# RWKV stage of a two-block network: small inverse blocks handled together, the identity added to a smaller tile, C's context left out, modulation slabs in fours

## The chip, the cores and the metric

The kernel runs on one core of a Trainium2 chip. The metric is the device time of one execution in microseconds (us): the median of three runs. Five engines work side by side, each through its own queue in order: TensorE (PE in the profile, its weight loads PEld), VectorE (DVE), ScalarE (ACT), GpSimd (POOL) and SyncE (SP), which here only issues loads of weights. They wait for one another by semaphores.

## The reference

Two transformer-like blocks over 512 tokens of width 1024, with a context of 256 tokens beside them. The first block normalises and modulates the tokens (a silu of `c` times `ada_w` gives six vectors: two for the first norm, four for later), multiplies tokens and context by one wide matrix `w_in`, and feeds the columns to two branches: an RWKV branch and a state-space branch (SSM). Then come a merge, a mixture of experts, and the second block. What the change touches:

```python
def step(s, inp):                       # rwkv_scan, for each token, 16 heads of 64, two directions
    r_t, w_t, k_t, v_t, kk_t, a_t = inp
    sa = jnp.einsum('bhvk,bhk->bhv', s, -kk_t)
    s = s * w_t[:, :, None, :] + sa[..., None] * (kk_t * a_t)[:, :, None, :] + v_t[..., None] * k_t[:, :, None, :]
    return s, jnp.einsum('bhvk,bhk->bhv', s, r_t)

# ssm_prep: convolution over x, B and C; C is read for outputs only
xbc = jax.nn.silu(dw_conv_centred(xbc, p['ssm_conv_w'], p['ssm_conv_b']))
xs, bm, cm = jnp.split(xbc, [SSM_DIM, SSM_DIM + SSM_BC], axis=-1)
```

The context gives states, no outputs: over it `rwkv_scan` and `ssd_chunked` are called with `with_output=False`, so C (`cm`) of the context enters nothing.

## The kernel before

**The RWKV branch** takes a chunk of 64 tokens at a time. Inside a chunk the state's correction is a triangular system, so each chunk, head and direction needs the inverse of a 64x64 unit-triangular matrix. There are 8 pairs of heads and 3 units a pair (context; tokens in two blocks, forward and backward in opposite order): 24 units of 16 matrices. A unit goes through three generators:

- `unit_in` prepares decays and the products AR and BK, multiplies them on PE (L1532), masks the result into G (L1537), **adds the identity to A's part of G, once for each direction (L1539)**, and writes A to a buffer in DRAM, `da`.
- `unit_inv` inverts. It reads the 64 diagonal 16x16 blocks of `da` back with one matrix to a partition (Ab), multiplies by a mask into Qb (L1571), and builds the inverse inside a partition on DVE for block sizes b = 2, 4 and 8: for each diagonal block a product (L1579) and a sum (L1581), twice over: four instructions for each of 8/b blocks. Then `Qb` goes through DRAM back to a layout for PE, and two more levels (16 to 32, 32 to 64) are done with matmuls (L1632, L1639, L1654, L1662). Between the first two of these, a mask `lv` (which holds the identity too) is multiplied onto the product: Yl (L1636).
- `unit_chain` runs the state through four chunks: for each, PE, then P (DVE, L1700), PE, W (ACT, L1708 and L1709), PE, then Sall (DVE, L1727).

**The order of the work.** PE's and SP's queues follow the order in which the program is written; on DVE, ACT and POOL a planner with costs of its own sorts. The program goes in 26 steps, numbered -2 to 23. Step i interleaves the chain of unit i, the inverse of unit i+1 and the inputs of unit i+2 with a list of fills, in 12 rounds; in each round every stream gives a twelfth of its work. A stream's work is the sum of what its `yield`s give, as a share of its weight:

```python
while at < n - 1 and sum(load[:at + 1]) >= total * (at + 1) // n:
    at += 1
steps[at].append(f(p))
load[at] += w
```

Fills, in order, with weights: 20 convolution tiles `conv_in` (24 each), the two halves of the remaining modulation `adaln_rest` (84 each), 5 more convolution tiles, and 16 gate tiles (16 each). The seven later head pairs (64 each) are bound to steps 0, 3, 6 and so on. A fill is mostly `in_proj`: for each of 8 slices of the contraction three matmuls of 512 columns (tokens; L202, L205 and L206, into `d`), and where the context is wanted three of 256 (into `dc`). Tiles 20 to 23 of `conv_in` are C.

**Modulation.** Each half has 32 matmuls (L1207) of a single weight column against a slab of 128x512 of `ada_w`. Four results share a PSUM bank, at partitions 0, 32, 64 and 96. A slab is loaded by SP (L1206) into a ring of five buffers `wr`, which the other fills use too. After each matmul comes a `yield 2.6`.

Of the kernel before, what the change touches and what calls it, by code (L numbers as in the profile page):

```python
# [15 lines left out]
AX = mybir.AxisListType  # L16
PSUM = bass.MemoryType.PSUM
P = 128
# [1014 lines left out]
L, CT = 512, 256  # L1033
N = L + CT
CH = 64
# [14 lines left out]
HE = [dict(A="",P="gpsimd",V="vector")[x] for x in "AAAP"]  # L1050
YS, YC, SG, SI, KS = 1.5, .6, 44, 20, 0
HQ = 6
EYE = 0
SH = 0
XA = 1

# [4 lines left out]
def host_consts1():  # L1061
    f = np.float32
    out = {}
    i = np.arange(P)
    p, t = i[:, None] % 64, np.arange(64)[None, :]
    one = lambda c: np.broadcast_to(c, (P, c.shape[1])).astype(f)
    out["rw"] = np.concatenate([one(p < t), one(p <= t), one(p > t), one(p >= t)], 1)
    out["eye2"] = one(p == t)
    pp, tt = i[:, None] % 32, np.arange(32)[None, :]
    lv = [(pp // 16 == 0) & (tt // 16 == 1) | (pp == tt), (pp // 16 == 1) & (tt // 16 == 0) | (pp == tt)]  # L1070
    out["lv"] = np.concatenate(lv, 1).astype(f)
    e = np.arange(16)
    out["q2"] = one(((e[:, None] == e[None, :]) | (e[:, None] % 2 == 0) & (e[None, :] == e[:, None] + 1)).reshape(1, 256))
    out["half16"] = np.stack([i // 16 % 2 == 0, i // 16 % 2 == 1], 1).astype(f)
    out["half32"] = np.stack([i // 32 % 2 == 0, i // 32 % 2 == 1], 1).astype(f)
    out["blk64"] = (i[:, None] // 64 == i[None, :] // 64).astype(f)
    k, j = i[:, None], i[None, :]
    for nm, m in (("le", k <= j), ("ge", k >= j), ("gt", k > j), ("lt", k < j)):
        out["m_" + nm] = m.astype(f)
    r = np.ones((1, 256), f)  # L1080
    r[:, ::CH] = 0
    out["rst"] = np.broadcast_to(r, (P, 256)).astype(f)
    return out
# [10 lines left out]
class Block1(Block2):  # L1094
# [100 lines left out]
    def adaln_rest(self):  # L1195

        nc, t = self.nc, self.t
        self.mod = self.dram.tile([8, 512], F32, name="mod")

        def half(p, h):  # L1200
            ps = self.pd.tile([P, 512], F32, name="d", bufs=2)
            for k in range(KC):
                for g in range(4):
                    w = self.raw()
                    c0 = 2048 + h * 2048 + g * 512
                    nc.sync.dma_start(w, t["ada_w"][0, k * P:(k + 1) * P, c0:c0 + 512])  # L1206
                    i = nc.tensor.matmul(ps[32 * g:32 * g + 1], self.sT[:, k, 0:1], w, start=(k == 0), stop=(k == KC - 1))  # L1207
                    if self.last is not None:
                        self.paced(i)
                    self.latest = i  # L1210
                    yield 2.6
            for g in range(4):
                m = p.tile([P, N + 3], F32, name="u", bufs=2)
                nc.scalar.copy(m[32 * g:32 * g + 1, :512], ps[32 * g:32 * g + 1])
                nc.gpsimd.dma_start(self.mod[h * 4 + g:h * 4 + g + 1], m[32 * g:32 * g + 1, :512])
        return [(84, lambda p: half(p, 0)), (84, lambda p: half(p, 1))]

    def bcast(self, out, ap, off, n, eng=None):
        (eng or self.nc.gpsimd).dma_start(out, bass.AP(tensor=ap.tensor, offset=ap.offset + off, ap=[[0, P], [1, n]]))
# [240 lines left out]
    def unit_in(self, p, q, pr, u, un):  # L1460

        nc, cs = self.nc, self.cs
# [10 lines left out]
        for j, src in enumerate((xw, xa)):  # L1473
            for d, ps in enumerate(pss):
                rd = slice(64 * d, 64 * d + 64)
                tk = slice(blocks[d] * U, (blocks[d] + 1) * U)
                i = nc.tensor.matmul(ps[:, j * U:(j + 1) * U], lw[rd, j], src[rd, tk], start=True, stop=True)
# [46 lines left out]
        G = p.tile([P, 2, 4, 2, 2, CH], F32, name="G", bufs=3)  # L1524
# [3 lines left out]
        for d in range(2):  # L1528
            pss = [q.tile([P, 4, 2, CH], F32, name="g", bufs=2) for _ in hs]
            for c in range(4):  # L1530
                for ps, r in zip(pss, hs):
                    i = nc.tensor.matmul(ps[:, c, :na], BK[r, d, c].rearrange("p s t -> p (s t)"),  # L1532
                                         AR[r, d, :na, c * CH:(c + 1) * CH], start=True, stop=True)
            self.mark(i)
            yield 4
            for h, ps in enumerate(pss):
                nc.vector.tensor_mul(G[:, d, :, h, :na], ps[:, :, :na], mk[:, d, None, :na].to_broadcast([P, 4, na, CH]))  # L1537
            Ad = G[:64, d, :, :, 0].rearrange("p c h t -> p (c h) t")
            (nc.gpsimd if EYE else nc.vector).tensor_add(Ad, Ad, self.k["eye2"][:64, None].to_broadcast([64, 8, CH]))  # L1539
            ps = q.tile([P, 4, P], F32, name="g", bufs=2)  # L1540
            for c in range(4):
                i = nc.tensor.transpose(ps[:, c], BK[:, d, c].rearrange("p s t -> p (s t)"), self.ident)
            self.mark(i)
            nc.scalar.copy(bk[:, d], ps)
            yield 2
# [15 lines left out]
    def unit_inv(self, p, q, pr, u, un, after):  # L1561
        nc = self.nc
# [5 lines left out]
        Ab, Qb, tm = AQ[:64, 0], AQ[:64, 1], AQ[64:].rearrange("p z a b -> p (z a b)")  # L1568
# [1 line left out]
        yield 1  # L1570
        nc.vector.tensor_mul(Qb, Ab, self.k["q2"][:64].rearrange("p (a b) -> p a b", a=16))  # L1571
        W = p.tile([P, 4, 32], F32, name="Vt")[:64].rearrange("p a b -> p (a b)")
        sq = lambda x, o, i, j, b: x[:, o + i:o + i + b, o + j:o + j + b]
        for b in (2, 4, 8):
            for o in range(0, 16, 2 * b):
                t4 = tm[:, :b * b * b].rearrange("p (i t j) -> p i t j", i=b, t=b)
                w = W[:, :b * b].rearrange("p (i t) -> p i t", i=b)
                for lhs, rhs, dst in ((sq(Ab, o, 0, b, b), sq(Qb, o, b, b, b), w), (sq(Qb, o, 0, 0, b), w, sq(Qb, o, 0, b, b))):
                    nc.vector.tensor_mul(t4, lhs[:, :, None, :].to_broadcast([64, b, b, b]),  # L1579
                                         rhs.rearrange("p j t -> p t j")[:, None].to_broadcast([64, b, b, b]))  # L1580
                    nc.vector.reduce_sum(dst, t4, axis=AX.X)  # L1581
            yield YJ
        nc.scalar.dma_start(view(db, 0, [[256, 64], [1, 256]]), Qb.rearrange("p a b -> p (a b)"))
        Qp = p.tile([P, 8, 16], F32, name="Qp")
# [4 lines left out]
        for d in range(2):  # L1589
            ps = q.tile([P, 2, P], F32, name="g", bufs=2)  # L1590
            for j in range(2):
                c = 4 * self.BLOCKS[u][d] + 2 * j
                i = nc.tensor.transpose(ps[:, j], pr.vT[:, c * CH:(c + 2) * CH], self.ident)
            self.mark(i)
            for b in range(2):
                o = V[64:, 3 - b::-2, d] if d else V[64:, b::2, d]
# [3 lines left out]
        ps = q.tile([P, 4, 2, CH], F32, name="g", bufs=2)  # L1600
        for n in range(4):
            for d, c in ((0, n), (1, 3 - n)):
                for h in range(2):
                    i = nc.tensor.matmul(ps[hs[h], n, d], un.G[64:, d, c, h, 0], V[64:, n, d, h], start=True, stop=True)
# [13 lines left out]
        H = 32  # L1618
# [9 lines left out]
        lv = self.k["lv"].rearrange("p (d t) -> p d t", d=2)  # L1628
        all_ = [(g, d, c) for d in range(2) for c in range(4) for g in range(4)]
        ps = q.tile([P, 2, 4, H], F32, name="t", bufs=1)  # L1630
        for a in all_:
            i = nc.tensor.matmul(pk(ps, *a), blk((T1, T0)[a[1]], *a), Qg(*a), start=True, stop=True)  # L1632
        self.mark(i)
        yield 2
        Yl = p.tile([P, 2, 4, H], F32, name="Yl")
        nc.vector.tensor_mul(Yl, ps, lv[:, :, None].to_broadcast([P, 2, 4, H]))  # L1636
        ps = q.tile([P, 2, 4, H], F32, name="t", bufs=1)
        for a in all_:
            i = nc.tensor.matmul(pk(ps, *a), Tg(*a), pk(Yl, *a), start=True, stop=True)  # L1639
# [100 lines left out]
    def spills(self):  # L1740

        nc = self.nc
        self.sg = self.dram.tile([16, P, L], F32, name="sg1")
        self.sz = self.dram.tile([16, P, L], F32, name="sz1")
        self.su = self.dram.tile([25, P, N], F32, name="su1")

        def stage(p):
            return p.tile([P, N + 3], F32, name="u", bufs=2)

        def gate(p, i, z):  # L1750
            def ev(ps):
                g = p.tile([P, L], F32, name="u", bufs=2)
                nc.scalar.activation(g, ps, AF.Tanh, scale=0.5)
                if z:
                    nc.vector.scalar_tensor_tensor(g, g, 1.0, ps, op0=OP.add, op1=OP.mult)
                else:
                    nc.vector.tensor_scalar(g, g, 0.5, 0.5, op0=OP.mult, op1=OP.add)
                nc.gpsimd.dma_start((self.sz if z else self.sg)[i], g)
            yield from self.in_proj((SS if z else GT) + i * P, P, ev)

        def conv_in(p, m):
            n = P if m < 24 else 64
            u = stage(p)[:, :N]
            yield from self.in_proj(SS + 2048 + m * P, n, lambda ps: nc.scalar.copy(
                u[:n, CT:].rearrange("p (c r) -> p c r", r=8), ps.rearrange("p (r c) -> p c r", r=8)),
                lambda ps: nc.scalar.copy(u[:n, :CT], ps))
            nc.gpsimd.dma_start(self.su[m, :n], u[:n])
        self.zs, self.gates = ([lambda p, i=i, z=z: gate(p, i, z) for i in range(16)] for z in (True, False))
        early = (self.zs + self.gates)[:NZ]
        self.late = (self.zs + self.gates)[NZ:]  # L1770
        return [(24, lambda p, i=i: conv_in(p, i)) for i in range(25)] + [(16, f) for f in early]


    def exp_small(self, p, x, name):
# [901 lines left out]
```

## Time and profile before

| | |
|---|---|
| median of 3 runs | 4425.99 us (4418.01 to 4428.55) |
| profiled execution: its own time | 4428.13 us |
| profiled execution: span | 4426.3 us |
| PE busy | 4059.9 us, 92% |
| DVE busy | 2266.0 us, 51% |
| ACT busy | 1576.9 us, 36% |
| POOL busy | 1005.9 us, 23% |
| mean granted TensorE clock | 0.961 |

The profile is one execution. In the windows of [rows 2] the first is the whole RWKV stage from the chain of unit 0 on, the others are steps 2, 5, 11, 13, 14 and 22, each from the first matmul of its chain to that of the next. A busy share counts the time in which an instruction of that engine ran; of the clock, the profile gives the share of full speed that TensorE was granted in a stretch. Line numbers are those of the kernel before. An fp32 matmul stands as two records in the trace, one for each pass.

### The profile page before, as it was taken

What the parts mean: (1) busy time and instruction counts of PE and PEld (TensorE: products, weight loads), DVE (VectorE), ACT (ScalarE), POOL (GpSimd) and SP (SyncE); (2) the same over time, 40 slices, a digit from 0 to 9 for tenths busy, and PEclk for the clock granted to TensorE, in tenths of its full rate; (3) what the DMA queues carried; (4) which work ended last, traced back from release to release, by engine and by line L of the source; (5) the groups of instructions that cost most, each with busy time, mean ns of one, the idle gap of its engine ahead of it and who ended that gap; (6) DMA issues with size and microseconds to landing.
All of it is one profiled execution on the core that took longest, in us unless ns stands there. A gap on an engine that the chain in (4) does not pass through costs nothing. (4 is left out here: it accounts for less than half of the span.)

```text
span 4426.3 us, 70343 instructions
## 1 busy us (share of the span) xinstructions
PE 4059.9 (92%) x28255; PEld 2997.1 (68%) x28255; DVE 2266.0 (51%) x4106; ACT 1576.9 (36%) x3184; POOL 1005.9 (23%) x1320
## 2 busy tenths in 40 slices
PE   7889888788898888699998999999999999999998
PEld 5767665576665556543335777878888877878887
DVE  4666766757858875611113245565343245555332
ACT  3333322233336554200003564433232464433231
POOL 1333333233545542300001131230001131221000
PEclk9999998898999999899998999999999999999999
DMA  5222224322342335599996322343232322333332
GB/s 167 69 55 70 59 57 127 84 71 57 109 143 90 113 105 164 190 352 392 402 400 218 98 70 74 94 141 95 96 95 91 98 65 74 98 113 119 95 95 76
DMA packets 537490, 573.24 MB, mean 130 GB/s; under 512 B 127024, under 2 KB 427572, under 8 KB 536140
## 3 DMA queue, kind: packets, MB, share of 16 engines
q1 hardware_dynamic: 400940, 463.04, 31.4%
q0 software_dynamic: 23008, 75.62, 5.2%
q10 hardware_dynamic: 113216, 30.09, 3.3%
q8 instruction: 222, 3.64, 0.3%
q14 instruction: 104, 0.85, 0.1%
HBM read 508.40 MB, written 56.05 MB: 128 GB/s over the span
## 5 line engine op out<-in xcount | busy, mean ns | idle before, releaser
L202 PE MATMUL d<-hh,wh 128*128 128x512 f32 (+1 forms) x1952 | 856.3, 439 | 3.7 <-ACT wh L183 2.6
L205 PE MATMUL d<-hl,wh 128*128 128x512 f32 (+1 forms) x1952 | 779.2, 399 | 14.4 <-DVE hl L184 9.2
L206 PE MATMUL d<-hh,wl 128*128 128x512 f32 (+1 forms) x1952 | 778.1, 399 | 5.7 <-DVE wl L184 5.6
L184 DVE TENSOR_TENSOR wl<-wr,wh 128x1024 fp32r<-128x1024 f32 (+1 forms) x378 | 437.5, 1161 | 650.8 <-ACT wh L183 646.1
L183 ACT CAST wh<-wr 128x1024 fp32r<-128x1024 f32 (+2 forms) x509 | 433.6, 855 | 850.1 <-PE d L205 359.5
L202 PEld LDWEIGHTS d<-hh,wh 128*128 128x128 f32 x1952 | 377.0, 193 | 106.3 <-issue 38.8
L206 PEld LDWEIGHTS d<-hh,wl 128*128 128x128 f32 x1952 | 375.2, 192 | 96.2 <-DVE wl L184 9.6
L205 PEld LDWEIGHTS d<-hl,wh 128*128 128x128 f32 x1952 | 377.3, 193 | 91.6 <-issue 21.3
L184 POOL TENSOR_TENSOR wl<-wr,wh 128x512 fp32r<-128x512 f32 (+1 forms) x131 | 186.2, 1424 | 141.8 <-ACT wh L183 141.0
L202 PE MATMUL d<-wh,hh 128*128 128x256 f32 x704 | 204.5, 291 | 6.2 <-ACT wh L183 5.7
L202 PE MATMUL m<-wh,gh 128*128 128x512 f32 x512 | 200.0, 391 | 7.9 <-ACT wh L183 7.9
L205 PE MATMUL d<-wl,hh 128*128 128x256 f32 x704 | 202.2, 287 | 3.1 <-DVE wl L184 1.7
L206 PE MATMUL d<-wh,hl 128*128 128x256 f32 x704 | 201.4, 286 | 0.0
L205 PE MATMUL m<-wl,gh 128*128 128x512 f32 x512 | 200.1, 391 | 0.0
L206 PE MATMUL m<-wh,gl 128*128 128x512 f32 x512 | 199.7, 390 | 0.0
L1715 POOL TENSOR_SCALAR Sl<-Sall,lam 128x64 f32<-128x64 f32 x176 | 97.4, 565 | 202.2 <-DVE Sall L1727 201.8
L2532 PE MATMUL pa<-ew,XE 128*64 128x512 f32 x496 | 141.9, 608 | 0.0
L202 PEld LDWEIGHTS d<-wh,hh 128*128 128x128 f32 x704 | 136.3, 194 | 8.2 <-ACT wh L183 6.1
L205 PEld LDWEIGHTS d<-wl,hh 128*128 128x128 f32 x704 | 136.3, 194 | 3.9 <-DVE wl L184 2.1
L206 PEld LDWEIGHTS d<-wh,hl 128*128 128x128 f32 x704 | 136.2, 193 | 0.1
L2532 PE MATMUL pb<-ew,XE 128*64 128x512 f32 x504 | 128.2, 597 | 6.2 <-DMA ew<-in_exp_w_dram 6.2
L2532 PE MATMUL py<-ew,ec 128*64 128x512 f32 x512 | 130.5, 598 | 2.4 <-DMA ew<-in_exp_w_dram 2.4
(750 smaller groups left out, 8193.2 us busy)
## 6 DMA issues: line engine op xcount, KB each, us to landing
ew<-in_exp_w_dram SPq DMA_DIRECT2D x189, 1024.0 KB
wr<-in_w_ff_dram SPq DMA_DIRECT2D x128, 512.0 KB
wr<-in_w_in_dram SPq DMA_DIRECT2D x116, 512.0 KB
wr<-in_w_in_dram SPq DMA_DIRECT2D x167, 256.0 KB
wr<-in_ada_w_dram SPq DMA_DIRECT2D x64, 256.0 KB
sg<-gev POOLq DMA_DIRECT2D x48, 256.0 KB, 2.6
sgt<-sg POOLq DMA_DIRECT2D x48, 256.0 KB, 3.3
su<-u POOLq DMA_DIRECT2D x24, 384.0 KB, 3.2
```

Source lines behind the costliest of these rows:

```text
L183: i = self.high(hi, src)
L184: j = self.low.tensor_sub(lo, src, hi.bitcast(F32))
L202: i = nc.tensor.matmul(out, lh, rh, start=start, stop=False)
L205: nc.tensor.matmul(out, lh, rl, start=False, stop=False)
L206: self.latest = nc.tensor.matmul(out, ll, rh, start=False, stop=stop)
L1715: nc.gpsimd.tensor_scalar(Sl[:, d], S[:, d, n], lam[:, d, c:c + 1], None, op0=OP.mult)
L2532: nc.tensor.matmul(ps[c][64 * j:64 * j + 64], lhs(k + i, j), w_, start=(k + i == 0), stop=(k + i == KC - 1))
```

## The change

Four edits, and what follows from them:

- In `unit_inv` the blocks of one size are handled together: for b = 2 one product instruction for each column t, over all four blocks, and one sum for all; for the second product likewise, with a sum for each row i. For b = 4 and 8 the products stay one to a block, and the first sum is one for all blocks. The ones on Qb's diagonal, which came from the identity in A, are now set by a memset on POOL behind L1571.
- The identity isn't added to A in `unit_in`; `lv` holds no identity, and it is added to Yl, a tile of 128x256, after the mask.
- `conv_in` leaves out the context for tiles 20 to 23, and their weight is 16.
- `adaln_rest` takes four buffers, issues the four loads, then the four matmuls, then `yield 8`. A half's weight is 64.

The weights of the fills decide which step a fill falls into, so the list is cut at other places.

```diff
-    out["eye2"] = one(p == t)
-    lv = [(pp // 16 == 0) & (tt // 16 == 1) | (pp == tt), (pp // 16 == 1) & (tt // 16 == 0) | (pp == tt)]
+    out["eye"] = (pp == tt).astype(f)
+    lv = [(pp // 16 == 0) & (tt // 16 == 1), (pp // 16 == 1) & (tt // 16 == 0)]
...
             for k in range(KC):
-                for g in range(4):
-                    w = self.raw()
+                ws = [self.raw() for _ in range(4)]
+                for g, w in enumerate(ws):
                     c0 = 2048 + h * 2048 + g * 512
                     nc.sync.dma_start(w, t["ada_w"][0, k * P:(k + 1) * P, c0:c0 + 512])
+                for g, w in enumerate(ws):
                     i = nc.tensor.matmul(ps[32 * g:32 * g + 1], self.sT[:, k, 0:1], w, start=(k == 0), stop=(k == KC - 1))
...
-                    yield 2.6
+                yield 8
...
-        return [(84, lambda p: half(p, 0)), (84, lambda p: half(p, 1))]
+        return [(64, lambda p: half(p, 0)), (64, lambda p: half(p, 1))]
...
-            Ad = G[:64, d, :, :, 0].rearrange("p c h t -> p (c h) t")
-            (nc.gpsimd if EYE else nc.vector).tensor_add(Ad, Ad, self.k["eye2"][:64, None].to_broadcast([64, 8, CH]))
...
-        sq = lambda x, o, i, j, b: x[:, o + i:o + i + b, o + j:o + j + b]
+        nc.gpsimd.memset(bass.AP(tensor=Qb.tensor, offset=Qb.offset, ap=[list(Qb.ap[0]), [17, 16]]), 1.0)
+        def sq(x, i, j, b, by):
+            n = 8 // b
+            return bass.AP(tensor=x.tensor, offset=x.offset + 16 * i + j, ap=[list(x.ap[0]), [34 * b, n], *by])
         for b in (2, 4, 8):
-            for o in range(0, 16, 2 * b):
-                t4 = tm[:, :b * b * b].rearrange("p (i t j) -> p i t j", i=b, t=b)
-                w = W[:, :b * b].rearrange("p (i t) -> p i t", i=b)
-                for lhs, rhs, dst in ((sq(Ab, o, 0, b, b), sq(Qb, o, b, b, b), w), (sq(Qb, o, 0, 0, b), w, sq(Qb, o, 0, b, b))):
-                    nc.vector.tensor_mul(t4, lhs[:, :, None, :].to_broadcast([64, b, b, b]),
-                                         rhs.rearrange("p j t -> p t j")[:, None].to_broadcast([64, b, b, b]))
-                    nc.vector.reduce_sum(dst, t4, axis=AX.X)
+            n = 8 // b
+            t4 = tm[:, :n * b * b * b].rearrange("p (n i t j) -> p n i t j", n=n, i=b, t=b)
+            w = W[:, :n * b * b]
+            w4 = w.rearrange("p (n j t) -> p n j t", n=n, j=b)
+            def mul(lhs, rhs):
+                if n > b:
+                    for t in range(b):
+                        nc.vector.tensor_mul(t4[:, :, :, t], lhs, rhs[:, :, :, t][:, :, None].to_broadcast([64, n, b, b]))
+                else:
+                    for m in range(n):
+                        nc.vector.tensor_mul(t4[:, m], lhs[:, m, :, None].to_broadcast([64, b, b, b]),
+                                             rhs[:, m].rearrange("p j t -> p t j")[:, None].to_broadcast([64, b, b, b]))
+            part = lambda x, j: sq(x, 0, j, b, [[16, b], [1, b]])
+            mul(part(Ab, b), sq(Qb, b, b, b, [[16, b], [1, b]]))
+            nc.vector.reduce_sum(w, t4.rearrange("p n i t j -> p (n i t) j"), axis=AX.X)
+            mul(part(Qb, 0), w4)
+            o = part(Qb, b)
+            if n > b:
+                for i in range(b):
+                    nc.vector.reduce_sum(o[:, :, i], t4[:, :, i], axis=AX.X)
+            else:
+                for m in range(n):
+                    nc.vector.reduce_sum(o[:, m], t4[:, m], axis=AX.X)
             yield YJ
...
         nc.vector.tensor_mul(Yl, ps, lv[:, :, None].to_broadcast([P, 2, 4, H]))
+        nc.vector.tensor_add(Yl, Yl, self.k["eye"][:, None, None].to_broadcast([P, 2, 4, H]))
...
+            c = CT if 20 <= m < 24 else 0
...
-                lambda ps: nc.scalar.copy(u[:n, :CT], ps))
-            nc.gpsimd.dma_start(self.su[m, :n], u[:n])
+                None if c else lambda ps: nc.scalar.copy(u[:n, :CT], ps))
+            nc.gpsimd.dma_start(self.su[m, :n, c:], u[:n, c:])
...
-        return [(24, lambda p, i=i: conv_in(p, i)) for i in range(25)] + [(16, f) for f in early]
+        return [(16 if 20 <= i < 24 else 24, lambda p, i=i: conv_in(p, i)) for i in range(25)] + [(16, f) for f in early]
```

## Rows read from the trace of the kernel before

**Rows 1.** The page, part 1: busy us, share of the span, instructions.

```profile
PE 4059.9 (92%) x28255; PEld 2997.1 (68%) x28255; DVE 2266.0 (51%) x4106; ACT 1576.9 (36%) x3184; POOL 1005.9 (23%) x1320
```

**Rows 2.** Windows: bounds, us, busy PE, PEld, DVE, ACT, POOL, clock, DMA, GB/s.

```profile
165.17:1228.24 1063.07, 930.33 (x11981) 694.61 (x11975) 729.68 (x1724) 337.81 (x777) 396.45 (x591) 0.93 0.29 76
...
256.32:305.71 49.39, 44.47 (x578) 36.74 (x573) 25.77 (x65) 14.86 (x36) 17.77 (x26) 0.97 0.26 67
...
400.57:440.62 40.05, 35.96 (x529) 28.29 (x524) 25.81 (x65) 13.39 (x32) 13.32 (x23) 0.96 0.24 59
...
668.41:709.39 40.98, 36.22 (x498) 15.50 (x493) 24.76 (x63) 11.05 (x27) 7.70 (x16) 0.92 0.71 219
...
764.26:810.32 46.06, 39.75 (x530) 18.90 (x524) 25.58 (x69) 12.95 (x30) 12.59 (x20) 0.93 0.67 200
810.32:846.52 36.20, 25.01 (x434) 19.65 (x428) 27.93 (x65) 10.74 (x26) 11.13 (x24) 0.58 0.14 28
...
1180.58:1228.24 47.66, 37.54 (x490) 28.06 (x485) 45.28 (x86) 16.80 (x35) 25.38 (x37) 0.89 0.42 130
```

**Rows 3.** Waits of PE from 165 to 1225: us in total, times, longest.

```profile
PE p L1693 <- DVE P L1700: 25.8, 16, 3.5
...
PE p L1693 <- DVE Sall L1727: 16.5, 14, 3.0
```

**Rows 4.** Groups of DVE by line: busy us, mean ns of one, idle before.

```profile
L1579 DVE TENSOR_TENSOR AQ<-AQ 64x8 f32<-64x8 f32 x96 | 20.2, 210 | 3.3
...
L1581 DVE TENSOR_REDUCE Vt<-AQ 64x4 f32<-64x8 f32 x96 | 15.0, 156 | 3.3
...
L1539 DVE TENSOR_TENSOR G<-G,eye 64x512 f32<-64x512 f32 x48 | 33.6, 700 | 1.2
...
L1636 DVE TENSOR_TENSOR Yl<-t,lv 128x256 f32<-128x256 f32 x24 | 9.8, 409 | 20.0 <-PE t L1632 20.0
```

**Rows 5.** Timeline and one window around step 8: start, length, idle before in brackets.

```profile
530.31 0.54 DVE L1571 TENSOR_TENSOR AQ<-AQ,q 64x256 f32<-64x256 f32 x1
...
533.09 0.61 DVE L1667 SCALAR_TENSOR_TENSOR Q<-t,half,Q 128x128 f32<-128x128 f32 x2 [2.05 <-PE t L1662]
...
533.09:548.62 15.53, 12.20 (x126) 8.92 (x123) 14.27 (x41) 6.73 (x15) 4.22 (x8) 1.00 0.18 57
...
548.62 0.45 PE L1693 MATMUL p<-P,Q 64*64 64x64 f32 x8 [2.78 <-DVE P L1700]
...
530.10 1.83 POOL L1649 TENSOR_SCALAR Q<-Qe,half 128x256 f32<-128x256 f32 x2
...
568.81 0.10 POOL L1274 MEMSET u<- 128x1 f32 x1
...
501.40 1.27 POOL L184 TENSOR_TENSOR wl<-wr,wh 128x512 fp32r<-128x512 f32 x1 [2.54 <-ACT wh L183]
```

**Rows 6.** Modulation: its group, timeline pieces, and a window of its loads (last column GB/s).

```profile
L1207 PE MATMUL d<-wr,sT 128*1 128x512 f32 x128 | 40.4, 677 | 2.4 <-DMA wr<-in_ada_w_dram 2.3
...
674.71 1.03 PE L1207 MATMUL d<-wr,sT 128*1 128x512 f32 x4
...
703.98 1.03 PE L1207 MATMUL d<-wr,sT 128*1 128x512 f32 x6
...
33.95 4.54 PE L1176 MATMUL d<-aw,sz 128*32 128x512 f32 x40
...
673.77 0.33 SPq L1206 DMA_DIRECT2D wr<-in_ada_w_dram  x1
...
676.43 1.02 PE L1207 MATMUL d<-wr,sT 128*1 128x512 f32 x2 [0.69 <-DMA wr<-in_ada_w_dram]
...
688.00:700.00 12.00, 11.90 (x166) 1.00 0.89 272
```

**Rows 7.** Timeline: two matmuls over context columns, one after the other.

```profile
930.87 0.28 PE L205 MATMUL dc<-hl,wh 128*128 128x256 f32 x1
930.99 0.28 PE L206 MATMUL dc<-hh,wl 128*128 128x256 f32 x1
```

More of the change, by code (lines that the diff above doesn't have):

```diff
@@ L1052 @@
 HQ = 6
-EYE = 0
 SH = 0
```

## The prediction

> **What bounds the kernel now.** I read the page first, then the stage in which all three edits lie, cut into its steps (a windows view), then who TensorE waited for, then single instructions.
>
> The page puts TensorE (PE) at 92% of the span and VectorE (DVE) at 51% [rows 1]. The RWKV stage is 1063.07 us of it, PE busy 930.33 us, DVE 729.68 us, granted clock 0.93 [rows 2]. PE's order there is written by hand, so an instruction that waits holds up all behind it. The reader is to see in rows 2 that a step's time follows PE's fill where there is much, and not where there is little. Steps 2 and 5 carry the same RWKV work. Step 2 has a fill load of 72 and takes 49.39 us, step 5 has 48 and takes 40.05: 9.34/24 = 0.39 us for a unit of load. Step 14 has none, yet takes 36.20 us: PE is busy 25.01 us of it at a mean granted clock of 0.58, and DVE 27.93 us. So above a load of about 48 PE decides; below that the chain between the engines does.
>
> DVE's share in that chain: over the stage PE stood still 25.8 us for P and 16.5 us for Sall, both written by DVE [rows 3]. Step 8 shows how. From 533.09 to 548.62 us DVE is busy 14.27 of 15.53 us in 41 instructions, the rest being 0.03 us after each; it is full. In that queue the small instructions of the 16x16 inverses (L1579, L1581) stand ahead of the chain's, and PE waits 2.78 us for P [rows 5].
>
> **The change part by part.** Sums are made against the profiled run: 4428.13 us, span 4426.3. That is 2.1 us over the median, 4425.99.
>
> *Small blocks together (24 units).* For blocks of 2, 16 instructions become 7: four products and five sums go, at 0.210 and 0.156 us [rows 4], with 0.03 us after each: 4 x 0.240 + 5 x 0.186 = 1.89 us. The remaining ones are up to four times as long in elements, still few; I count no surcharge. Of the blocks of 4 one of eight instructions goes and another doubles: nothing. Blocks of 8 stay.
>
> *Identity.* Two additions at 0.700 us go; one of 128x256 comes. The trace has none like it; the nearest is the masking just before it, 0.409 us [rows 4]. That is -1.46 + 0.44 = -1.02 us. The new one stands between two groups of PE matmuls (L1632, L1639), so PE waits for it unless other matmuls lie between; the steps put two rounds there, and I count 0 (at worst 24 x 0.44 = 10.6 us). The old second one stood ahead of the transpose and the write of `da`, which the next step's first product L1571 reads; that may start 0.7 us earlier.
>
> *The ones by GpSimd (POOL).* New: after L1571 a memset on POOL, and all of the inverse behind it. A memset there takes 0.10 us [rows 5]. What stands ahead of it decides. In step 8 L1571 ended at 530.85 us while POOL was on Q until 531.93 (1.83 us from 530.10): 1.1 us of wait. But DVE then stood still 2.05 us anyway, for L1667 [rows 5], so there it costs nothing. Behind the waiting DVE instruction are L1667, P and Sall, and PE waits for those. Lower bound 0; upper bound one stuck split, 2.54 us idle for ACT and 1.27 us long [rows 5], say 3.9 us a unit, 94 us in all. I take 0.8 us, nearer to step 8, and half of it covered: 0.4 us.
>
> Together DVE loses 1.89 + 1.02 - 0.4 = 2.5 us a unit, 60 us in all. PE gets back only what it waits for. The removed 1.9 us stand in the full stretch, ahead of the late P and Sall, whose 42.3 us are 1.8 us a step with the round trip in them. I take 0.6 us a step, **-15 us**. The bounds are 0 and the whole 60.
>
> *Context of C.* 4 tiles x 8 x 3 = 96 matmuls of 256 columns go. At the full clock they start 0.12 us apart [rows 7]: 11.5 us of PE time, in steps 16 and 17. Four copies by ACT go too, and a third of four stores.
>
> *Fours.* Now a round issues two or three modulation matmuls in a row. Each is two passes in the trace, so these are rows of 4 or 6. The reader is to see that four passes take 1.03 us and six the same [rows 6]: different column groups run beside each other. So do four matmuls: at 33.95 us 40 passes take 4.54 us, 0.91 us for eight. The 128 passes cost 40.4 us in some 25 groups; 16 groups at the same price cost 26 us, 7 us less for each half.
>
> The price is the ring of five slabs. After a group only one slab of the next is there; three must be fetched into the slots just freed. One issued at 673.77 us released its matmul at 676.43: 2.66 us; the queue moves 272 GB/s when kept full [rows 6], so 262 KB take 0.96 us more for each further one. A period is 1.0 + 2.66 + 2 x 0.96 = 5.6 us, and seven of them 39 us. SP's queue holds only weights and the loads of `lw`, behind which nothing is due earlier. [...]
>
> *The redistribution.* The weights in the list sum to 1400 instead of 1472, so the planner of fills cuts elsewhere. Worked through its loop, these steps change: 2 from 72 to 48; 11 from 84 to 88 (one convolution tile and the first half); 13 from 84 to 0; 14 from 0 to 64 (second half); 16 from 48 to 32; 17 from 72 to 56; 19 from 32 to 48; 20 from 64 to 48; 21 from 48 to 64; 22 from 64 to 48.
> - Step 2: 24 x 0.39 = -9.3 us. Step 17: 16 x 0.39 = -6.2 us, which is half of C's matmuls (5.8 us) seen from the step.
> - Step 11: 9.3 for the tile, 7 less for fewer groups, and the fetches: 39 us wanted where 64/88 of some 43 us are given, 8 us late, half of it in waits that PE has anyway. **+6**.
> - Step 13, now empty: it keeps its RWKV work; going from 48 to nothing gave 40.05 - 36.20 = 3.9 us (steps 5 and 14): **-4**.
> - Step 14: eight groups with 39 us between first and last, and a round after: 42 us, **+6**.
> - 16 against 19 and 20 against 21 exchange 16 units each: 0. In 22 DVE is busy 45.28 of 47.66 us [rows 2], so PE's relief brings nothing.
>
> Sum -9.3 - 6.2 + 6 - 4 + 6 = **-7.5 us**; bounds -25 (no late fetch, step 13 ten us shorter) and +10 (every fetch fully late). Later stages get the same instructions.
>
> Total -15 - 7.5 = -22.5 us: 4405.6 us beside the profiled run, **4403 us** as a median.
>
> **Rivals.**
> 1. *DVE's whole relief arrives.* For it: the full stretch of step 8. Against: with a load of 64 and more PE decides. 60 us, 7.5 from the fills: 4426 - 67 = 4359; with the memset's 0.8 us uncovered 24 x 2.1 = 50 us, 4368, which I take.
> [...]
> 3. *The fours starve.* They don't run earlier, since the fourth slab comes late each time: a period of 7 us makes 49 us a half, 10 us more for each of steps 11 and 14, less 4 in cover: 4403 + 12 = 4415.
> 4. *The memset is the new wait, and the kernel gets slower.* Place: POOL's queue at the start of each inverse, behind a split that waits for ACT's cast. DVE's gain is 2.9 us a unit before it and the fills give 0.3; it decides from a mean wait of 3.2 us. Were DVE's time all on the path, 4.0 us a unit would make 24 x 0.8 = 19 us: 4445; 3.9 us of queue and 1.3 us (one more split) 24 x 2.0 = 48 us: 4474. Against: POOL is busy only 396.45 of the 1063.07 us [rows 2].
>
> **How the numbers follow.** Forecast 0.48, rival 1 0.17, rival 2 0.14, rival 3 0.09, rival 4 0.12. A difference under 0.3% (13 us) can't be told from none. Forecast's own range is 4388 to 4418. Faster by more than that: rival 1, most of the forecast (0.40) and a third of rival 3 and some of 2: 0.62. Slower: most of rival 4: 0.11. Same: 0.27. For 8 in 10 the range runs from between rival 1's two times, 4362, past rival 2 to 4434; below it lies a tenth at most, above it rival 4.
>
> **What would show it.** After: L1539 gone, small L1579/L1581 rows at 18 instead of 28 a unit; DVE busy in the stage lower by about 65 us; waits of PE for P and Sall at 25 to 30 us instead of 42.3; L1571's follower waiting for POOL under 1 us a unit (rival 4: over 3). `dc` loses 96 matmuls. Modulation passes in rows of 8 at about 1 us, with PE waits for `in_ada_w` of 5 to 10 us a half. [...] The prediction is wrong if the stage shrinks by over 50 us or grows.

## The result, and the profile after

| | before | after |
|---|---|---|
| median, four runs each on one chip | 4427.27 us | **4375.83 us** (4374.02 to 4382.55) |
| ratio | | 0.9891, interval 0.9873 to 0.9908 |
| profiled execution: own time, span | 4428.13, 4426.3 | 4374.02, 4372.2 |
| mean granted TensorE clock | 0.961 | 0.963 |

The kernel is 51 us faster; forecast was 23. One execution of a later run, e10's profiled one, took 12624.93 us at a mean granted clock of 0.427, and nothing is read from it. The page, part 1, after (it answers to [rows 1]; busy us, share, instructions):

```profile
PE 4040.2 (92%) x28137; PEld 2979.9 (68%) x28159; DVE 2181.1 (50%) x3842; ACT 1574.7 (36%) x3180; POOL 1013.1 (23%) x1344
```

Windows after, columns as in [rows 2], with one more step: the stage from the chain of unit 0 to that of unit 23, then steps 2, 5, 8, 11, 13, 14 and 22:

```profile
160.96:1171.52 1010.56, 909.62 (x11884) 675.03 (x11879) 643.26 (x1465) 336.65 (x774) 400.54 (x610) 0.94 0.30 78
248.87:285.60 36.73, 35.72 (x530) 28.01 (x524) 22.33 (x54) 13.59 (x32) 14.07 (x24) 0.95 0.25 64
374.38:410.15 35.77, 34.28 (x530) 27.04 (x524) 22.92 (x54) 13.38 (x32) 13.95 (x24) 1.00 0.25 66
502.45:538.21 35.76, 34.29 (x530) 27.04 (x525) 22.85 (x54) 13.37 (x32) 14.07 (x24) 1.00 0.26 67
629.28:684.81 55.53, 48.33 (x547) 24.51 (x541) 22.19 (x54) 12.19 (x30) 8.89 (x17) 0.91 0.56 171
735.46:772.07 36.61, 28.39 (x467) 23.88 (x461) 21.74 (x56) 9.96 (x25) 9.98 (x17) 0.67 0.12 22
772.07:813.99 41.92, 37.50 (x497) 15.61 (x492) 21.30 (x54) 11.41 (x28) 8.74 (x16) 0.92 0.70 213
1135.98:1171.52 35.54, 33.48 (x465) 24.68 (x461) 32.20 (x67) 13.56 (x29) 20.53 (x28) 0.87 0.31 94
```

The stage went from 1063.07 to 1010.56 us: 52.5 of the 54.1 us that the span lost. Two things are to be seen. First, step 5, whose fills did not change, went from 40.05 to 35.77 us. It is no exception: the 13 steps with the same list of fills lost 28.8 us, 2.2 us each in the mean, from 4.3 us less in step 5 to 3.1 us more in step 7. Second, the steps whose fills changed moved a lot, and against each other: 2 by -12.7 us, 13 by -9.5, 17 by -8.8, 22 by -12.1, but 11 by +14.6, 21 by +9.3 and 14 by +5.7. With 2.2 us taken off each, those ten sum to about -2 us. So the gain is these 2.2 us a step, and the new places of the fills sum to nearly nothing.

What PE waits for in the stage after (us in total, times, longest; it answers to [rows 3]):

```profile
PE t L1685 <- ACT Vt L1682: 18.4, 23, 5.5
PE p L1716 <- ACT W L1732: 15.7, 8, 3.7
PE d L1208 <- DMA wr<-in_ada_w_dram: 9.7, 10, 2.7
PE p L1716 <- DVE P L1723: 9.3, 9, 3.0
...
PE p L1716 <- DVE Sall L1750: 2.2, 5, 1.0
```

P and Sall cost 11.5 us instead of 42.3. What stands on top now is ScalarE's (the wait for Vt was 22.4 us before), and the fours' late slabs.

The modulation's group, which answers to the first line of [rows 6]:

```profile
L1208 PE MATMUL d<-wr,sT 128*1 128x512 f32 x128 | 41.4, 632 | 10.1 <-DMA wr<-in_ada_w_dram 9.7
```

In fours it costs PE no less than singly, 41.4 us instead of 40.4.

DVE's groups of the inverse (columns as in [rows 4]; the first line is of the kernel before):

```profile
L1579 DVE TENSOR_TENSOR AQ<-AQ,Vt 64x8 f32<-64x8 f32 x96 | 21.3, 222 | 3.2
...
L1659 DVE TENSOR_TENSOR Yl<-Yl,eye 128x256 f32<-128x256 f32 x24 | 12.2, 510 | 0.5
L1588 DVE TENSOR_TENSOR AQ<-AQ 64x16 f32<-64x16 f32 x48 | 11.8, 274 | 7.8 <-POOL AQ L1572 7.4
...
L1588 DVE TENSOR_TENSOR AQ<-AQ,Vt 64x16 f32<-64x16 f32 x48 | 8.7, 219 | 0.8
...
L1600 DVE TENSOR_REDUCE AQ<-AQ 64x8 f32<-64x16 f32 x48 | 5.8, 161 | 0.8
L1595 DVE TENSOR_REDUCE Vt<-AQ 64x16 f32<-64x32 f32 x24 | 4.4, 181 | 0.8
```

Twice the elements (64x16 instead of 64x8) cost 0.274 and 0.219 us instead of 0.210 and 0.222, four times as many in a sum 0.181 instead of 0.156: what an instruction costs here is mostly its being there.

The full stretch of step 8 after, its timeline on DVE with the window over it, answers to [rows 5]:

```profile
502.63 0.61 DVE L1690 SCALAR_TENSOR_TENSOR Q<-t,half,Q 128x128 f32<-128x128 f32 x2 [1.76 <-PE t L1685]
503.27 0.18 DVE L1595 TENSOR_REDUCE Vt<-AQ 64x16 f32<-64x32 f32 x1
503.49 0.29 DVE L1723 TENSOR_TENSOR P<-p,PV 128x128 f32<-128x128 f32 x1
...
515.06 0.28 DVE L1723 TENSOR_TENSOR P<-p,PV 128x128 f32<-128x128 f32 x1
...
502.63:515.06 12.43, 11.93 (x125) 8.90 (x123) 11.91 (x30) 6.26 (x15) 3.12 (x5) 1.00 0.19 60
```

DVE is still full, 11.91 of 12.43 us. But the stretch is shorter: its second P starts 12.43 us after Q's product. Before, it started 15.18 us after (533.09 to 548.27).

### The profile page after: what moved, and what is told of

The parts are those of the page before. It is cut to its first block, busy times and chain, and to the rows that moved or that the text cites. A ratio compares the mean times of both kernels' runs of the same rounds, so it can differ in the third digit from the quotient of the medians.

```text
span 4372.2 us, 69947 instructions
## 1 busy us (share of the span) xinstructions
PE 4040.2 (92%) x28137; PEld 2979.9 (68%) x28159; DVE 2181.1 (50%) x3842; ACT 1574.7 (36%) x3180; POOL 1013.1 (23%) x1344
## 3 DMA queue, kind: packets, MB, share of 16 engines
q8 instruction: 222, 3.64, 0.3%
HBM read 508.39 MB, written 55.53 MB: 129 GB/s over the span
## 5 line engine op out<-in xcount | busy, mean ns | idle before, releaser
L202 PEld LDWEIGHTS d<-hh,wh 128*128 128x128 f32 x1952 | 378.2, 194 | 107.9 <-issue 40.4
```

The costliest lines, as they stand in the source:

```text
L202: i = nc.tensor.matmul(out, lh, rh, start=start, stop=False)
```

## The experiments

The first four tell apart which part pays. Theory 1: VectorE's relief arrives whole and the fills give nothing (the prediction's rival 1 without its 7.5 us from the fills). Theory 2: the prediction's split. Theory 3: the parts help one another.

**e1: the inverse alone** (small blocks, identity, memset; slabs and C as before).

```diff
 # against the changed kernel: the fills' two edits undone
-                ws = [self.raw() for _ in range(4)]
...
-            c = CT if 20 <= m < 24 else 0
```

> Only the inverse is changed (small blocks together, identity on Yl, ones by GpSimd); modulation and C's context as before. Theory 1 (DVE's whole relief arrives, the fills' edits sum to about nothing): the unchanged-load steps of the changed kernel are 2.2 us shorter each, so 24 x 2.2 = 53 us less: 4374 us, and PE's waits for P and Sall together near 12 us instead of 42. Theory 2 (the split of the prediction: DVE 15 us, the fills the rest, 36 us): 4412 us. Theory 3 (the two parts only help together, since each alone leaves the other as the bound): 4420 us or more here and in the next run both.

4377.27 us, ratio 0.988 (0.9863 to 0.9897): all of the gain. Its stage, and who PE waits for there:

```profile
158.23:1177.32 1019.09, 929.38 (x11980) 695.60 (x11975) 646.73 (x1466) 340.53 (x779) 406.16 (x614) 0.92 0.30 78
...
PE p L1714 <- DVE Sall L1748: 9.5, 6, 3.6
...
PE p L1714 <- DVE P L1721: 6.7, 7, 1.7
```

PE works as long as before (929.38 against 930.33 us); summed over all rows of the waits view, its waits fell from 131.5 to 89.2 us, which is the stage's 44 us but for 2. P and Sall are some 25 of these 42 us (42.3 to 16.2 by their rows); the rest came off waits for other writers.

**e2: the fills alone** (C and the fours on the kernel before), **e3: the fours alone**, **e4: C alone.** The edits are the diff's parts in `half` and in `conv_in`, with their weights.

```diff
 # e3: half() as in the change        # e4: conv_in() as in the change
+                ws = [self.raw() for _ in range(4)]
...
+            c = CT if 20 <= m < 24 else 0
```

> Only C's context left out and modulation in fours, with the redistribution that follows; the inverse as before. Theory 1: 4425 us, same as before within 0.3%. Theory 2: 4391 us. Theory 3: 4420 us or more.

> Only modulation in fours (weight 64 for 84 a half, so the fills are cut elsewhere). Theory 1 with late loads: the waits of PE for slabs of ada_w were 9.7 us in the changed kernel (2.3 before) and steps 11 and 14 grew by 14.6 and 5.7 us, so about 8 us slower than before: 4435 us. Rival (fewer groups save PE time): 4417 us.

> Only C's context left out, weights 16 for 24. 96 matmuls at 0.12 us are 11.5 us of PE time in two steps. Theory 1: 10 us faster, 4417 us, since PE decides in those steps. Rival (clock or chain take it back): within 3 us of before, 4426 us.

e2: 4428.05 us, ratio 0.9998 (0.9985 to 1.0011). e3: 4434.05, 1.0017 (1.0009 to 1.0026). e4: 4425.07, 0.9988 (0.9977 to 0.9998). So on the kernel before the fours cost some 6 us, C gives some 3, and both together nothing. Theory 2 falls. Theory 1 stands for the sum; e7 will show that theory 3 may have a part in it. That C gives so little here is to be seen in the stage of e4:

```profile
162.94:1225.43 1062.49, 918.64 (x11884) 682.71 (x11878) 729.13 (x1723) 337.49 (x774) 392.63 (x591) 0.92 0.29 75
```

PE's busy time fell by 11.7 us, as costed, and the stage by 0.6: PE waits for others instead, 142.3 us in all where it was 131.5.

**e5: the small blocks alone; e6: the identity and the memset alone.**

```diff
 # e5: loops of the change in the inverse, L1539 kept, no memset
 # e6: loops of before, and
-            (nc.gpsimd if EYE else nc.vector).tensor_add(Ad, Ad, ...)
+        nc.gpsimd.memset(...)
+        nc.vector.tensor_add(Yl, Yl, ...)
```

> The kernel before with the small blocks of a level together, and nothing else: the identity stays in A (two additions a unit), no memset. 24 x 1.9 us of DVE time go, 46 us. Theory 1 (DVE's time is worth some three quarters of itself here, as 51 us for about 68 in the inverse-only kernel): 34 us faster, 4394 us. Rival (only these instructions stand in the full stretch, the identity's gain is nothing): 50 us faster, 4378 us.

> The kernel before with the identity added to Yl for A and the ones set by a memset on GpSimd; the inverse's loops as before. DVE loses 1.40 us a unit and gains 0.5; the memset's wait is 0.3 us a unit. Theory 1: three quarters of 24 x 0.9, less what of the wait is not covered: 15 us faster, 4413 us. Rival (the identity lies outside the full stretch, and the memset and the longer way over Yl eat it): 4428 us or slower.

e5: 4378.1 us, ratio 0.9878 (0.9857 to 0.9899): everything. e6: 4429.07, 1.0001 (0.9989 to 1.0013): nothing, although it took 20 us of work off DVE in the stage. The stage of e5, then stage and waits of e6:

```profile
157.42:1155.20 997.78, 910.30 (x11981) 682.91 (x11975) 656.59 (x1488) 337.60 (x778) 406.78 (x587) 0.94 0.31 80
...
164.00:1230.29 1066.29, 923.03 (x11981) 689.01 (x11975) 709.75 (x1706) 339.74 (x781) 398.91 (x614) 0.94 0.29 76
...
PE p L1692 <- DVE P L1699: 24.7, 17, 3.3
...
PE p L1692 <- DVE Sall L1726: 16.9, 13, 3.0
...
DVE AQ L1577 <- POOL AQ L1570: 9.9, 19, 1.8
```

In e6 P and Sall are as late as ever. Where the additions stood tells why. DVE in step 8 of the kernel before, further on than [rows 5]:

```profile
548.27 0.29 DVE L1700 TENSOR_TENSOR P<-p,PV 128x128 f32<-128x128 f32 x1
...
553.61 0.68 DVE L1539 TENSOR_TENSOR G<-G,eye 64x512 f32<-64x512 f32 x1
554.28 0.29 DVE L1700 TENSOR_TENSOR P<-p,PV 128x128 f32<-128x128 f32 x1
...
559.43 0.48 DVE L1727 SCALAR_TENSOR_TENSOR Sall<-p,lam,Sl 128x64 f32<-128x64 f32 x2 [2.14 <-PE p L1693]
...
561.99 0.68 DVE L1539 TENSOR_TENSOR G<-G,eye 64x512 f32<-64x512 f32 x1
```

The small blocks lie between a step's first and second P (533.92 and 548.27 there); the identity lies after the second, where DVE soon stands idle 2.14 us for PE. So it is in the whole stage of that trace: of the 368 instructions on 64x8 elements 324 start between a step's first and second P and the other 44 after its fourth, while of the 44 additions none starts between the first two, and 35 start after the third. I measured the distance from the first P of a step to its second in each trace, as the mean of the 23 steps. It is 15.0 us in the kernel before and in e4, 14.8 in e6; and 13.3 in e1, 13.3 in e5, 13.1 in the changed kernel. Against the kernel before, these three are 1.7 to 1.9 us shorter, nearly all of the 1.9 us (e1) to 2.2 us (the change) by which a step got shorter.

**e7: the changed kernel without the fours; e8: the fours with half of the loads** (each group fetches two slabs and uses each twice).

```diff
 # e7: half() as before          # e8:
-                ws = [self.raw() for _ in range(4)]
-                for g, w in enumerate(ws):
+                ws = [self.raw() for _ in range(2)] * 2
+                for g, w in enumerate(ws[:2]):
```

> The changed kernel with modulation as before (single slabs, weight 84). Theory 1 with late loads (fours cost 6 us alone): 4370 us, 6 us faster than the changed kernel. Rival (with the inverse shortened the fours' fewer groups pay): 4380 us.

> The changed kernel, but each group of four modulation matmuls loads two slabs and uses each twice; half of ada_w's columns are left out. If late slabs are the fours' price, PE's waits for ada_w fall from 9.7 us (and 31 us of its weight loads') to under 3 and the time falls by 8 us or more: 4367 us. Rival (the price is where the fills are cut, step 13 empty and step 11 full): steps 11 and 13 as in the changed kernel, 4374 us or more.

e7: **4361.35 us**, ratio 0.984 (0.9822 to 0.9858), 14 us below the changed kernel by the medians (some 20 by the two ratios). It is e1 with C's matmuls gone, and 16 us below e1, the two intervals just apart: C, worth 3 us alone, brings its 11.5 us of PE and perhaps some more once the chain is shorter. The fours, 6 us alone, cost 14 here. So in the presence of the inverse both fills seem to count for more, with opposite signs, and their sum stays near zero.

e8: 4352.09, 0.9815 (0.9801 to 0.983). PE's wait for slabs falls from 9.7 to 0.3 us. The price of the fours is in their loads, then; but e8 is also 9 us below e7, so half of the loads is worth more than that price. Is the price in the bursts?

**e11: slabs in pairs.**

```diff
+                for g0 in (0, 2):
+                    ws = [self.raw() for _ in range(2)]
...
+                    yield 4
```

> The changed kernel with the modulation's slabs in twos (two fetched, two used, a yield of 4 after each two) where it has them in fours. If the price of the fours is that four slabs are late at once in a ring of five, pairs cost about what single slabs do: 4362 us (4355 to 4368). If the price is the number of matmuls that stand together, half of the price stays: 4369 us. If it is the budget of the yields, which is the same for pairs and fours (64 a half), nothing is gained: 4376 us.

4378.01 us, ratio 0.988 (0.986 to 0.99): the same as fours. So four slabs late at once cost no more than two, within the scatter. Two things set pairs and fours apart from single slabs: slabs come in groups, and a half weighs 64 in the list of fills. The traces show how the weight acts beside C's tiles of 16. With 84 the first half has step 11 for itself; with 64 the planner moves a convolution tile from step 5 into step 11, ahead of the half, and the second half from step 13 to step 14. From e7 to the changed kernel, step 5 lost 8.8 us by it (44.55 to 35.77), step 11 gained 13.7, and steps 13 and 14 together 7.7 (70.86 to 78.54). In sum that is 12.6 of the 14.9 us by which the stage got longer. Some of these may be the clock's: e7's profiled execution, 4353.16 us at a mean granted clock of 0.967, lies 8 us under its median, and its others had 0.961 to 0.963. Steps 5 and 11 in e7, then step 11 in e8; then, with fours, the stretch of the first half's passes and how it begins (the whole step stands above):

```profile
370.72:415.27 44.55, 42.94 (x579) 35.38 (x573) 23.64 (x54) 15.06 (x36) 17.14 (x27) 1.00 0.27 74
...
637.02:678.87 41.85, 34.47 (x497) 14.74 (x492) 20.65 (x51) 11.20 (x28) 8.45 (x15) 1.00 0.75 222
```

```profile
631.07:669.69 38.62, 37.66 (x546) 23.11 (x540) 21.34 (x51) 12.70 (x31) 9.09 (x16) 0.91 0.49 141
```

```profile
646.77:682.10 35.33, 28.77 (x328) 9.87 (x328) 6.82 (x15) 3.48 (x10) 4.15 (x7) 0.95 0.73 229
...
646.77 1.04 PE L1208 MATMUL d<-wr,sT 128*1 128x512 f32 x8
...
652.11 3.64 PE L1208 MATMUL d<-wr,sT 128*1 128x512 f32 x6 [2.74 <-DMA wr<-in_ada_w_dram]
```

With fours the half starts 17.5 us into the step (629.28 to 646.77), and 17.5 + 35.3 us and a rest of 2.7 make the 55.53 us shown above. From its first to its last modulation pass this first half takes 34.8 us before, 36.4 in e7 (singly), 34.3 in pairs, 35.4 in fours, and 18.5 in e8.

The grouping has a price of its own, though, and e3 shows it. There C's tiles still weigh 24, and a weight of 64 leaves the two halves alone in steps 11 and 13, where they are in the kernel before. Yet these steps took 48.22 and 50.00 us instead of 40.98 and 46.06, and PE waited 11.7 us for slabs instead of 2.3:

```profile
667.20:715.42 48.22, 37.27 (x497) 16.43 (x492) 24.67 (x63) 11.00 (x27) 8.05 (x16) 0.93 0.66 196
...
PE d L1209 <- DMA wr<-in_ada_w_dram: 6.7, 7, 1.8
```

The two halves take 42.8 and 40.8 us there, the longest of all traces. So fours alone cost some 11 us in these two steps, and the other steps of e3 gave 5 us back. How the price of the fours in the changed kernel divides between grouping and place isn't shown; fours at a weight of 84, which would tell, were not run.

**e9: the first product of the largest block twice; e10: levels 2 and 4 of the inverse left out.** These ask whether e1's rate, almost all of VectorE's relief, holds beyond the change.

```diff
 # e9
+            for _ in range(2 if b == 8 else 1):
                 mul(part(Ab, b), sq(Qb, b, b, b, [[16, b], [1, b]]))
 # e10, in the loop over b
+            if b < 8:
+                yield YJ
+                continue
```

> The changed kernel, with the first product of the largest block (64x512, 1.21 us of VectorE in its trace) computed twice in each unit; the result is the same. VectorE gets 1.24 us more per unit with the gap, 30 us over 24 units. If nearly all of VectorE's time in a unit reaches the end (the theory after the first eight runs: about 0.85 of it), the time is 4376 + 25 = 4401 us (4392 to 4410), and the units with unchanged load take about 1.1 us more each. If the prediction's split held (a quarter of it arrives), 4383 us (4378 to 4389).

> The changed kernel with the block levels 2 and 4 of the inverse left out (its output is then not the reference's): 16 instructions of VectorE fewer in each unit, 3.3 us busy and some 0.8 us of gaps and of the wait for the memset, so about 85 to 95 us over 24 units. If VectorE still sets the pace after the change as it did before, at 0.85 of its relief, the time is about 4300 us (4290 to 4315). If the change has used up what VectorE held back, and TensorE's own 910 us of work in the stage is the floor now, the time is above 4345 us.

e9: 4387.34 us, ratio 0.9907 (0.9888 to 0.9927): 11 us by the medians for 21 us of work more in the stage, in the range that I gave for the prediction's split and below the one for the high rate. Its interval overlaps that of the changed kernel (0.9873 to 0.9908), so the 11 us are not clear of the scatter. Its distance from first to second P is 13.6 us, half a microsecond up for a product of 1.15. e10: ratio 0.9854 (0.9831 to 0.9877), median 4368 of four executions, 8 us below the changed kernel where the rate promised 75; here too the intervals overlap. So there is no constant rate, and theory 1 holds for this cut, not as a rule: before the change the small blocks' time was uncovered; after it most of what is left of the inverse seems to lie beside something else. What that is, ACT's W and Vt at the head of the waits or PE's own work, isn't settled.

**e12: small blocks and C, without the identity, the memset and the fours.**

> The kernel before with two parts of the change alone: the small blocks of a level together, and C not projected for the context; the identity stays in its old place, there is no memset, and the slabs go singly. If the identity's move is worth nothing beside the small blocks as it is alone, and the parts add up, the time is that of the small blocks alone less 3 us: 4375 us (4365 to 4380), above the kernel without fours (4361 us). If the memset costs more than the move of the identity gives, it is below: 4350 us. If the move of the identity pays only once the small blocks are together, it is 13 us above the kernel without fours.

4366.75 us, ratio 0.9859 (0.9839 to 0.9879). Against e5 C brings 11 us here by the medians and 8 by the ratios, against 16 in e7 over e1. But the interval overlaps those of both e5 and e7, and the time lies between the expected outcomes: what the identity's move is worth beside the small blocks stays open, within about 10 us. e7 is the fastest complete kernel of those run.

## Why the prediction missed by half

- **The step that failed** is "I take 0.6 us a step, -15 us". The inverse measured 1.9 us a step (e1) to 2.2 (the change), some 50 us in all (e1: 4428.35 to 4377.27). The place was right: "the removed 1.9 us stand in the full stretch, ahead of the late P and Sall". By that sentence nearly all of the 1.9 us comes off the distance between the two P's, and so it did (15.0 to 13.1). What I did then was to scale by a wait total, 42.3 us or 1.8 us a step, as if only a third of a wait could be won. But 30.8 of those 42.3 us went, and in e1 waits for other writers fell too. The time, 4376 us, lies in the range for 8 in 10 (4362 to 4434) but below the forecast's own (4388 to 4418), and the prediction's own sign of being wrong, a stage that shrinks by over 50 us, came: 52.5.
- **Rival 1**, put at 4368 us with a chance of 0.17, is the case that came as far as VectorE goes: its 50 us arrived, without its 7.5 from the fills. What I held against it, "with a load of 64 and more PE decides", did not hold: of the 13 steps with the same fills the seven that carry a head pair (64) lost 2.3 us each, the six others 2.1.
- **VectorE's own sums** were near. The blocks of 2 gave 2.0 us a unit: 16 instructions of 71.5 us in all became 7 of 30.7, and nine gaps went (predicted 1.89). The blocks of 4, put at nothing, gave 0.5: 47.9 us became 36.7. L1570's product (L1571 before) fell from 0.732 to 0.446 us, which I had not foreseen; why it did isn't shown. DVE's busy time in the stage fell by 86 us; I had said about 65.
- **The identity**: the addition to Yl takes 0.510 us (0.44 predicted). The whole part is worth nothing on the kernel before (e6); it stood where DVE had time. I had counted its 1.02 us with the small blocks' as one relief, without asking of each where it stood.
- **The memset**: DVE's wait behind it is 7.2 us in 17 times over the stage, 0.3 us a unit; 0.8 was taken, under 1 us announced. Rival 4 falls.
- **C's matmuls**: 96 went, 344 to 312 of each of the three kinds of `dc`, at the cost counted. They brought 3 us on the kernel before (e4), and on top of the inverse 16 (e7 against e1) or 8 to 11 (e12 against e5). So PE's 11.5 us seem to pay in full only where VectorE's part comes with them.
- **The fills' places**: steps 2 (-12.7) and 17 (-8.8) went as said with the 2 us of DVE on top, 13 (-9.5) by 3 us more, and 14 (+5.7) was near. Step 11 was put at +6 and cost +14.6: I gave the tile 24/88 of 43 us, 12 us, and covered half of what the loads were late; the half began 17.5 us into the step and took 35.3 us more. Steps 20, 21 and 22 were put at nothing and moved by -7.6, +9.3 and -12.1. Sum -7.5 predicted; e2 says -0.3, and the changed kernel against e1 -1.4, both within the scatter.
- **The fours**: eight passes take 1.04 us, as said. A period, 5.6 us in the sum, was 4.8 for the first half, (680.12 - 646.77)/7 between the first passes of the first and the eighth group, and 4.6 for the second. The 5.6 us were an estimate from one slab's 2.66 us and the queue's 272 GB/s. Pairs and single slabs keep nearly the same pace (34.3 and 36.4 us from the first pass of the first half to its last, where fours take 35.4), and in e3 the period is 5.5 and 5.3 us; what sets it isn't shown. Rival 3's period of 7 us did not come. The 7 us that the fours were to save PE in each half did not come (41.4 us instead of 40.4 for both, where the sum had 26): the slabs of a group do not arrive together (PE waits for one 10 times, 9.7 us in all), and a group falls apart, as in the first half after 652.11, where 6 passes take 3.64 us.
- **Rival 2**, with a chance of 0.14, is that the granted clock takes back what the fills give; no run shows that. Step 13, now empty, went from a clock of 0.93 to 0.67, but became 9.5 us shorter (46.06 to 36.61 us); steps 15 and 16 moved by +1.0 and -1.9 us.

## What to carry to other kernels

A cut on an engine in the middle of a chain is worth what it takes off the distance between two links of that chain: look up, for each removed instruction, whether the next link waits behind it in the queue or whether the engine goes idle soon after. Scaling by a total of waits hides this. Such a gain ends where the next wait begins, so its rate can't be carried further (e10), but work on another engine that was hidden may then begin to pay (C: 3 us alone, 8 to 16 on top). Where a fill is bound by its loads, the weight that places it has to stand for these: a half took 34 to 43 us in the traces above with the full loads, and 18.5 with half of them (e8).

## What the runs showed of the hardware

In e5 the time goes largely with the granted clock: its five runs went from 4354.93 us at 0.966 to 4386.01 us at 0.958. So 0.008 of clock went with 31 us, over half of what the change gives. It is not the clock alone: two runs of e1, both at 0.964, are 13 us apart. Single traces carry this too: e7 and e12 do the same matmuls in the stage, and PE is busy 899.44 us of it at 0.95 in the one and 923.41 at 0.92 in the other. So single runs of two kernels tell little apart.
